# Attention in steps of two query tiles, the last output tile in two banks, and one warm-up matmul moved

## The chip, the cores and the metric

The kernel runs on one core of a Trainium2 chip. A core has a matmul engine (TensorE, PE in the profile, with its weight loads shown as PEld), a vector engine (VectorE, DVE), an activation engine (ScalarE, ACT), a general engine (GpSimd, POOL) and queues that start DMA transfers (SP's above all, shown as SPq; ACT and POOL start some too). Every engine works through its own list of instructions in order and waits at semaphores for the others. Matmul results go to PSUM, eight banks of 128 x 512 float32 here.

The metric is the device time of one execution in microseconds. The median of three runs is 651.36 (651.11 to 651.37).

## The reference

One layer of a hybrid encoder trunk in float32, one sequence of 512 rows of width 2048. One input projection gives q (8 heads of 128), k and v (2 heads each), a gate for attention, and the input and gate of a linear recurrence. Both groups are normed, gated and joined, and one output projection with a residual closes the layer.

```python
def attention_group(q, k, v, q_norm_w, k_norm_w):
    ...
    q = apply_axial_rope(rms_norm(q, q_norm_w), tables)
    k = apply_axial_rope(rms_norm(k, k_norm_w), tables)
    def block(qb):                      # 128 query rows, all heads
        s = jnp.einsum('bkgqd,bksd->bkgqs', qb, k_t) * scale
        p = jax.nn.softmax(s, axis=-1)
        return jnp.einsum('bkgqs,bksd->bkgqd', p, v_t)
...
def lru_group(xr, conv_w, conv_b, ...):  # convolution, gates, scan forward and back
    return (h_fwd + h_bwd).astype(xr.dtype)
...
# out = x + concat(norm(attn) * gate, norm(lru) * gate) @ w_out
```

## The kernel before

**Precision.** Every operand of a large product is split into a high and a low part, and each product is three matmuls (`mm3`, lines 146 to 148: high by high, high by low, low by high), so a 128 x 512 tile that sums over eight blocks takes 24 matmuls of 512 columns.

**Banks.** The eight PSUM banks are two rotating sets of four: `mm()` for scores, transposes, values and half of the outputs, `pj()` for projections and the other half of the outputs. A tile takes the bank that the tile four takes earlier in its set has used, and PE's first matmul into it waits until that older tile has been read.

**Stages.** First the input projection for the recurrence (`proj_feat`, lines from 286), then q, k and v, with the recurrence in between. Then attention, in which the projections for the gates run as filler: `weave(fill, attention(rots))` takes one step of `attention` and then as many filler pieces as it yields. One filler piece is six matmuls of 128 x 512. After attention, six more pieces and a sum of squares over heads (`group_rstd`, its matmuls at line 657). At the end the output projection, a scheme of seven products per group of columns.

**Start.** While the first chunk of x and of w_in arrives, PE is kept busy by matmuls on a tile of ones, 128 x 256 in bfloat16 (`busy`, line 942): `WARM` of them ahead of the transpose of norm_w (line 180), `WARM1` behind it, then the four transposes of x (line 233), then `WARM2`, then the first matmuls of the projection (line 294).

**Attention.** A query tile t of head h takes: `weights` (scores by `mm3`, maximum on DVE at line 576, exponential with its sum on ACT at line 579, reciprocal on DVE, scaling on POOL at line 581), `turn_weights` two steps later (four transposes at line 588, read out by ACT at line 590 and by DVE at line 591), and, one step after a head's last turn, `values` (12 matmuls, read out by DVE at line 602, squared by ACT at line 607 and summed by POOL at line 608). `turned` turns the q of the head after next (four transposes at line 536). Each step ends with `yield STEPS`, two filler pieces. Into attention also fall, among the fillers, the gates: `gate` calls four sigmoids on ACT (line 642) for each of two groups of four tiles.

PE and POOL follow the order of the code in attention; the lists of ACT, DVE and SP are set there by a scheduler. In the output stage PE, ACT, DVE and SP follow the code.

**Output.** `outputs` goes through two column groups g, each in two passes (P1, Q6, Q5, Q7, and then P2, Q3, Q4), over eight blocks i of the sum, with two tiles s of 128 rows for each product. For i from 0 to 5 the products take turns; the last two blocks are done product by product, so each product ends on its own. `take` hands banks out in turns: four from `mm`, four from `pj`. `done` reads a finished tile on DVE into the residual and stores it. The last tile of all is Q4, s = 1 of g = 1: it is read in two halves of 256 columns (line 893), both after its last matmul, and both are stored from SP's queue. Q7's tiles, in pj banks, are read at lines 877 and 879.

Of the kernel before, what the change touches and what calls it, by code (L numbers as in the profile page):

```python
# [18 lines left out]
SEQ = 512  # L19
DM = 2048  # L20
KT = DM // P
NT = SEQ // P
HD = 128
NH = 8
NKV = 2
G = NH // NKV
# [11 lines left out]
AHEAD = 600  # L38


WARM, WARM1, WARM2 = 9, 1, 4


STEPS = 2


H = 256
# [9 lines left out]
def hybrid_kernel(  # L57
# [20 lines left out]
    nc = tc.nc  # L78
# [44 lines left out]
    def b4(dt=F32, shape=(P, 2, SEQ)):  # L123
        pool, _, n = work()
        return pools[pool].tile(list(shape), dt, tag="b4", bufs=n, name=nm("b4"))
# [16 lines left out]
    def f(ap):  # L142
        return ap.bitcast(F32)
# [388 lines left out]
    def turn(rot, h):  # L532

        pt = mm()
        for t in range(NT):
            nc.tensor.transpose(pt[:, t * P : (t + 1) * P], rot[t][:, h, :], ident)  # L536
        return pt

    def split_ps(pt, hi, lo):
        nc.scalar.copy(hi, pt)  # L540
        nc.vector.tensor_sub(lo, pt, f(hi))
# [21 lines left out]
    def turned(rot, h):  # L563

        q = b4(F32R)
        split_ps(turn(rot, h), q[:, 0, :], q[:, 1, :])
        return q[:, 0, :], q[:, 1, :]

    def weights(q, g, t):

        qh, ql = q
        tt = slice(t * P, (t + 1) * P)
        sc = mm()
        mm3(sc, qh[:, tt], ql[:, tt], kth[g], ktl[g], True, True)
        mx = pools["att"].tile([P, 1], F32, tag="mx", bufs=16, name=nm("mx"))
        nc.vector.tensor_reduce(mx, sc, axis=AX.X, op=ALU.max, negate=True)  # L576
        p = k2()
        sm = pools["att"].tile([P, 1], F32, tag="sm", bufs=16, name=nm("sm"))
        nc.scalar.activation(p, sc, AF.Exp, bias=mx, accum_out=sm)
        nc.vector.reciprocal(sm, sm)  # L580
        nc.gpsimd.tensor_scalar(p, p, sm, 0.0, op0=ALU.mult, op1=ALU.add)
        return p

    def turn_weights(p, t, pth, ptl):
        tt = slice(t * P, (t + 1) * P)
        pt = mm()
        for s in range(NT):
            nc.tensor.transpose(pt[:, s * P : (s + 1) * P], p[:, s * P : (s + 1) * P], ident)  # L588
        p3 = pt.rearrange("p (s q) -> p s q", q=P)
        nc.scalar.copy(pth[:, :, tt], p3)  # L590
        nc.vector.tensor_sub(ptl[:, :, tt], p3, f(pth[:, :, tt]))

    def values(h, pth, ptl):

        gs = slice(h // G * HD, (h // G + 1) * HD)
        o = mm()
        for s in range(NT):
            mm3(o, vh[s][:, gs], vl[s][:, gs], pth[:, s, :], ptl[:, s, :], s == 0, s == NT - 1)
        if h % 2 == 0:
            ap_[h // 2] = aring.tile([P, 2, SEQ], F32, name=nm("av"))  # L600
        av, asum = ap_[h // 2][:, h % 2, :], sums["a"]
        nc.vector.tensor_copy(av, o)
        if h == 0:
            nc.scalar.activation(asum, av, AF.Square)
        else:
            sq = k2()
            nc.scalar.activation(sq, av, AF.Square)
            nc.gpsimd.tensor_add(asum, asum, sq)

    def attention(rots):  # L610

        qs, ps_, pts = {h: turned(rots[0], h) for h in range(2)}, {}, {}
        yield 13
        last = NH * NT
        for i in range(last + 3):
            h, t = divmod(i, NT)
            if i < last:
                ps_[i] = weights(qs[h], h // G, t)
                if t == 0 and h + 2 < NH:
                    qs[h + 2] = turned(rots[(h + 2) // G], (h + 2) % G)  # L620
            j = i - 3
            if j >= 0 and j % NT == NT - 1:
                values(j // NT, *pts.pop(j // NT))
            j = i - 2
            if 0 <= j < last:
                h, t = divmod(j, NT)
                if t == 0:
                    pts[h] = [
                        pools["att"].tile([P, NT, SEQ], F32R, tag="pt", bufs=ATT_PT, name=nm("pt"))
                        for _ in range(2)  # L630
                    ]
                turn_weights(ps_.pop(j), t, *pts[h])
            yield STEPS


    def gate(gs, pairs, row, sig):
# [39 lines left out]
    P1, Q6, Q5, Q7, P2, Q3, Q4 = (0, 0), (5, 5), (4, 3), (3, 4), (2, 2), (6, 1), (1, 6)  # L676
# [123 lines left out]
    PASS = (((0, "P1"), (5, "Q6"), (4, "Q5"), (3, "Q7")), ((2, "P2"), (6, "Q3"), (1, "Q4")))  # L800
    TAIL, PIECES, LAST_USE = 2, 13, 22
# [35 lines left out]
    def store(g, t, j, part=slice(0, SEQ), queue=None):  # L837

        cs = slice(j * SEQ + part.start, j * SEQ + part.stop)
        os_ = slice(2 * g * SEQ + cs.start, 2 * g * SEQ + cs.stop)  # L840
        (queue or nc.gpsimd).dma_start(of[t * P : (t + 1) * P, os_], xts[g][t][:, cs])
# [3 lines left out]
    def outputs(work):  # L845

        bank, tmp, at, held = {}, {}, [0], []

        def take(key):
            bank[key] = pj() if at[0] % 8 >= 4 else mm()  # L850
            at[0] += 1
            return bank[key]

        def tm(tag, s):
            tmp[tag, s] = fin_ev()
            return tmp[tag, s]

        def fin_ev():
            return pools["fin"].tile([P, SEQ], F32, tag="ev", bufs=4, name=nm("ev"))

        def done(g, name, s):

            xt = xts[g]
            b00, b01 = xt[s][:, :SEQ], xt[s][:, SEQ:]
            b10, b11 = xt[2 + s][:, :SEQ], xt[2 + s][:, SEQ:]
            v = nc.vector
            if name == "P1":
                nc.scalar.copy(tm("a", s), bank[name, s])
                v.tensor_add(b11, b11, tmp["a", s])
            elif name == "Q6":  # L870
                v.tensor_sub(tm("b", s), bank[name, s], tmp["a", s])
                v.tensor_sub(b01, b01, tmp["b", s])
            elif name == "Q5":
                v.tensor_add(tm("c", s), bank[name, s], tmp["b", s])
                v.tensor_add(b00, b00, tmp["c", s])
            elif name == "Q7":
                v.tensor_add(b00, bank[name, s], b00)
                store(g, s, 0)
                v.tensor_sub(b01, b01, bank[name, s])
                held.append((b10, tmp["c", s]))  # L880
            elif name == "P2":
                v.tensor_add(b11, bank[name, s], b11)
                store(g, 2 + s, 1)
            elif name == "Q3":
                v.tensor_add(b10, bank[name, s], b10)
                store(g, 2 + s, 0, queue=nc.sync if g else None)
            elif g == 0 or s == 0:
                v.tensor_add(b01, bank[name, s], b01)
                store(g, s, 1, queue=nc.sync if g else None)
            else:  # L890
                for h in range(2):
                    hs = slice(h * H, (h + 1) * H)
                    v.tensor_add(b01[:, hs], bank[name, s][:, hs], b01[:, hs])  # L893
                    store(g, s, 1, hs, nc.sync)

        def mult(use, s):

            g, second, k, i = use
            a, name = PASS[second][k]
            ah, al = mixed[i][1]  # L900
            bh, bl = ready[use]
            ts_ = slice(s * P, (s + 1) * P)
            if i == 0:
                take((name, s))
            for j, (lh, rh) in enumerate(((ah, bh), (ah, bl), (al, bh))):
                nc.tensor.matmul(  # L906
                    bank[name, s], lh[:, a, ts_], rh, start=i == 0 and j == 0,
                    stop=i == 7 and j == 2,
                )
            if i == 7:  # L910
                done(g, name, s)

        for n, use in enumerate(order_):
            g, second, k, i = use
            prepare(n + NW - 1)
            if (second, k, i) == (0, 0, 3):
                xts.setdefault(g, None)
                xts[g] = xts[g] or residual_tiles()
                residual(g)
            if second and k and held:  # L920
                b10, c = held.pop(0)
                nc.vector.tensor_add(b10, b10, c)
            if n * PIECES // LAST_USE != (n - 1) * PIECES // LAST_USE:
                next(work, None)
            if i < 8 - TAIL:
                for s in range(2):
                    mult(use, s)
            elif i == 7:
                for s in range(2):
                    for m in range(8 - TAIL, 8):  # L930
                        mult((g, second, k, m), s)

# [34 lines left out]
    for step in proj_feat(C_XR, a1, first, given):  # L969
# [8 lines left out]
        c, e = step  # L978
# [37 lines left out]
    rots = []  # L1016
# [150 lines left out]
```

## Time and profile before

| | |
|---|---|
| median of three runs | 651.36 us |
| profiled execution | 651.15 us |
| its span, first to last instruction | 649.4 us |
| PE busy | 644.0 us, 99% |
| DVE busy | 482.9 us, 74% |
| ACT busy | 345.8 us, 53% |
| POOL busy | 95.4 us, 15% |
| granted clock of PE | 1.000 |

The profile is one execution. Its span is the time from the first to the last instruction; the execution's own time is 1.8 us longer. Rows of the timeline give the start, the busy time, the engine, the line, the operation, the tiles (out<-in, without numbers) and their shape, with "x4" for four instructions in one row, and in square brackets the idle time ahead and what ended it. A matmul's busy time overlaps that of the next, so the time it costs is read from the distance of the starts, or from the chain of waits, whose rows give a start, the time it adds, and the engine and line.

### The profile page before, as it was taken

To read this page: it belongs to the slowest core of one execution; us is meant where nothing else is said; L and a number is where in the kernel's file an instruction comes from. 1 tells how busy PE (TensorE), PEld (TensorE's weight loads), DVE (VectorE), ACT (ScalarE), POOL (GpSimd) and SP (SyncE) were. 2 spreads that over 40 slices of the span, in tenths; PEclk is the share of its full clock that TensorE was granted. 3 is DMA by queue.
4 is the path that set the end of the run, shared out by engine and by line. 5 is a ranking of instruction groups with operands and counts; after the bars stand their busy time and mean duration, and the time that the engine had idled before them with its cause. 6 is when DMAs were issued, how large, how long until landed. Compare 5 with 4: busy or idle time off the path is not lost.

```text
span 649.4 us, 8581 instructions
## 1 busy us (share of the span) xinstructions
PE 644.0 (99%) x2955; PEld 532.6 (82%) x2955; DVE 482.9 (74%) x829; ACT 345.8 (53%) x639; POOL 95.4 (15%) x127
## 2 busy tenths in 40 slices
PE   9999999999999999999999999999999999999997
PEld 7888888888888888888888888888888888888885
DVE  5878679977688925855956668539967978699994
ACT  3533799489856615454744446435444754443441
POOL 0000000000012312132442435411000000010000
PEclk9999999999999999999999999999999999999999
DMA  8933243322334331446775778673354957586322
GB/s 294 323 102 111 66 138 97 98 66 66 94 101 134 97 112 33 120 139 150 173 185 142 195 145 194 152 158 92 119 174 162 333 166 247 194 280 212 119 94 97
DMA packets 53068, 96.96 MB, mean 149 GB/s; under 512 B 4317, under 2 KB 14689, under 8 KB 52897
## 3 DMA queue, kind: packets, MB, share of 16 engines
q1 hardware_dynamic: 45264, 75.17, 36.8%
q0 software_dynamic: 7056, 20.72, 13.8%
q10 hardware_dynamic: 704, 0.53, 0.3%
q8 instruction: 23, 0.38, 0.2%
q14 instruction: 21, 0.16, 0.1%
HBM read 92.21 MB, written 20.98 MB: 174 GB/s over the span
## 4 chain that ended last, share of the span: by engine, by line
PE 99%; DVE 0%; DVEq 0%; issue 0%; POOL 0%; POOLq 0%
PE pj L146 20%; PE pj L147 20%; PE pj L148 20%; PE mm L906 13%; PE pj L906 10%; PE mm L148 3%; PE mm L147 3%; PE mm L146 3%; PE mm L588 2%; PE mm L233 1%; PE pj L294 1%; PE mm L536 1%; PE mm L942 1%; PE mm L657 0%; DVE xt L893 0%; DVEq L1163 0%
## 5 line engine op out<-in xcount | busy, mean ns | idle before, releaser
L146 PE MATMUL pj<-x,wh 128*128 128x512 f32 x376 | 150.9, 401 | 0.0
L148 PE MATMUL pj<-x,wl 128*128 128x512 f32 x376 | 146.8, 390 | 0.0
L147 PE MATMUL pj<-x,wh 128*128 128x512 f32 x376 | 146.8, 390 | 0.0
L206 ACT CAST wh<-wr 128x512 fp32r<-128x512 f32 x143 | 85.5, 618 | 72.0 <-PE pj L148 25.0
L207 DVE TENSOR_TENSOR wl<-wr,wh 128x512 fp32r<-128x512 f32 x144 | 99.3, 711 | 31.0 <-ACT wh L206 31.0
L148 PEld LDWEIGHTS pj<-x,wl 128*128 128x128 f32 x376 | 70.6, 188 | 15.5
L146 PEld LDWEIGHTS pj<-x,wh 128*128 128x128 f32 x376 | 70.7, 188 | 13.8
L147 PEld LDWEIGHTS pj<-x,wh 128*128 128x128 f32 x376 | 70.8, 188 | 13.3
L720 ACT CAST oh<-rw 128x512 fp32r<-128x512 f32 x94 | 56.2, 620 | 36.7 <-PE mm L906 17.1
L146 PE MATMUL pj<-wh,x 128*128 128x512 f32 x192 | 75.0, 391 | 0.0
L147 PE MATMUL pj<-wl,x 128*128 128x512 f32 x192 | 74.8, 389 | 0.0
L148 PE MATMUL pj<-wh,x 128*128 128x512 f32 x192 | 74.8, 389 | 0.0
L721 DVE TENSOR_TENSOR ol<-rw,oh 128x512 fp32r<-128x512 f32 x94 | 61.7, 688 | 10.3 <-ACT oh L720 8.9
L906 PE MATMUL mm<-ol,mh 128*128 128x512 f32 x128 | 49.8, 389 | 0.0
L906 PE MATMUL mm<-oh,ml 128*128 128x512 f32 x128 | 49.8, 389 | 0.0
L906 PE MATMUL mm<-oh,mh 128*128 128x512 f32 x128 | 49.8, 389 | 0.0
L590 ACT CAST pt<-mm 128x512 fp32r<-128x512 f32 x32 | 18.7, 586 | 53.6 <-PE mm L588 53.6
L146 PEld LDWEIGHTS pj<-wh,x 128*128 128x128 f32 x192 | 36.0, 188 | 7.6
L148 PEld LDWEIGHTS pj<-wh,x 128*128 128x128 f32 x192 | 36.1, 188 | 7.6
L147 PEld LDWEIGHTS pj<-wl,x 128*128 128x128 f32 x192 | 36.1, 188 | 7.3
L576 DVE TENSOR_REDUCE mx<-mm 128x1 f32<-128x512 f32 x32 | 22.1, 690 | 24.3 <-PE mm L148 24.0
L906 PE MATMUL pj<-oh,ml 128*128 128x512 f32 x96 | 37.4, 389 | 0.0
(211 smaller groups left out, 1106.5 us busy)
## 6 DMA issues: line engine op xcount, KB each, us to landing
wr<-in_w_in_dram SPq DMA_DIRECT2D x71, 512.0 KB, 3.7
rw<-in_w_out_dram SPq DMA_DIRECT2D x63, 256.0 KB, 3.7
ts<-in_w_out_dram POOLq DMA_DIRECT2D x24, 512.0 KB, 6.6
rw<-ts SPq DMA_DIRECT2D x31, 256.0 KB, 4.6
ts<-ts POOLq DMA_DIRECT2D x8, 512.0 KB, 5.3
xt<-in_x_dram SPq DMA_DIRECT2D x8, 512.0 KB, 9.4
b<-in_x_dram SPq DMA_DIRECT2D x7, 512.0 KB, 8.7
out_dram<-xt POOLq DMA_DIRECT2D x12, 256.0 KB, 3.3
```

The lines of the kernel that those rows point to most:

```text
L146: nc.tensor.matmul(acc, lh, rh, start=start, stop=False)
L147: nc.tensor.matmul(acc, lh, rl, start=False, stop=False)
L148: nc.tensor.matmul(acc, ll, rh, start=False, stop=stop)
L206: rounded(hi, raw[:, k, :])
L207: nc.vector.tensor_sub(lo, raw[:, k, :], f(hi))
L233: nc.tensor.transpose(pt[:, t * P : (t + 1) * P], xc[:, t, ks], ident)
L576: nc.vector.tensor_reduce(mx, sc, axis=AX.X, op=ALU.max, negate=True)
L588: nc.tensor.transpose(pt[:, s * P : (s + 1) * P], p[:, s * P : (s + 1) * P], ident)
L590: nc.scalar.copy(pth[:, :, tt], p3)
L720: nc.scalar.copy(hi, src)
L721: nc.vector.tensor_sub(lo, src, f(hi))
L906: nc.tensor.matmul(bank[name, s], lh[:, a, ts_], rh, start=i == 0 and j == 0, stop=i == 7 and j == 2,)
```

## The change

Three parts.

1. `WARM, WARM1` go from 9, 1 to 10, 0: the warm-up matmul that stood between the transpose of norm_w and the transposes of x stands ahead of both.
2. Attention goes in steps d of two query tiles. A step does the values of a head whose turns are complete (even d from 4 on), then the turns of two tiles of weights from the step before last, then in odd d up to 11 the turn of q, then a score tile, one filler piece, a score tile, three filler pieces. The last values yield no filler; 85 pieces lie within attention instead of 83, and six instead of eight after the last values.
3. The last output tile is summed in two banks of 256 columns each: half 0 in the mm bank of the tile before, half 1 in the next bank in turn, a pj bank. Each matmul of 512 columns becomes two of 256 with the same weights. Within the last two blocks half 0 comes first, so it is complete six matmuls ahead of half 1. Half 0 is stored from SP's queue, half 1 from ACT's.

```diff
-WARM, WARM1, WARM2 = 9, 1, 4
-STEPS = 2
+WARM, WARM1, WARM2 = 10, 0, 4
+STEPS = 1, 3
...
-        last = NH * NT
-        for i in range(last + 3):
-            h, t = divmod(i, NT)
-            if i < last:
-                ps_[i] = weights(qs[h], h // G, t)
-                if t == 0 and h + 2 < NH:
-                    qs[h + 2] = turned(rots[(h + 2) // G], (h + 2) % G)
-            j = i - 3
-            if j >= 0 and j % NT == NT - 1:
-                values(j // NT, *pts.pop(j // NT))
-            j = i - 2
...
-                turn_weights(ps_.pop(j), t, *pts[h])
-            yield STEPS
+        for d in range(2 * NH + 3):
+            h, half = divmod(d - 4, 2)
+            if h >= 0 and half == 0:
+                values(h, *pts.pop(h))
+            h, half = divmod(d - 2, 2)
+            if 0 <= h < NH:
...
+                for t in (2 * half, 2 * half + 1):
+                    turn_weights(ps_.pop((h, t)), t, *pts[h])
+            h, half = divmod(d, 2)
+            if h < NH:
+                if half == 1 and h + 2 < NH:
+                    qs[h + 2] = turned(rots[(h + 2) // G], (h + 2) % G)
+                for e, t in enumerate((2 * half, 2 * half + 1)):
+                    ps_[h, t] = weights(qs[h], h // G, t)
+                    yield STEPS[e]
+            elif d < 2 * NH + 2:
+                yield sum(STEPS)
+            else:
+                yield 0
...
-            else:
-                for h in range(2):
-                    hs = slice(h * H, (h + 1) * H)
-                    v.tensor_add(b01[:, hs], bank[name, s][:, hs], b01[:, hs])
-                    store(g, s, 1, hs, nc.sync)
+                hs = slice(half * H, (half + 1) * H)
+                v.tensor_add(b01[:, hs], bank[name, s, half][:, :H], b01[:, hs])
+                store(g, s, 1, hs, (nc.sync, nc.scalar)[half])
...
+            if half is None:
+                key, to, cols = (name, s), slice(0, SEQ), slice(0, SEQ)
+            else:
+                key, to, cols = (name, s, half), slice(0, H), slice(half * H, (half + 1) * H)
             if i == 0:
-                take((name, s))
+                take(key)
             for j, (lh, rh) in enumerate(((ah, bh), (ah, bl), (al, bh))):
                 nc.tensor.matmul(
-                    bank[name, s], lh[:, a, ts_], rh, start=i == 0 and j == 0,
+                    bank[key][:, to], lh[:, a, ts_], rh[:, cols], start=i == 0 and j == 0,
...
+            for s in range(2):
+                last = g == 1 and PASS[second][k][1] == "Q4" and s == 1
+                for half in (0, 1) if last else (None,):
+                    for m in range(8 - TAIL, 8) if i == 7 else (i,) if i < 8 - TAIL else ():
+                        mult((g, second, k, m), s, half)
```

The code that follows the first changed lines stands four or more lines further down, so that line 906 before is line 913 after, and lines 877 and 879 are 881 and 883.

On PE in attention, before, ahead of the fifth score tile's fillers: a score tile (`mm_568`), the turn of q into `mm_573`, one turn of weights into `mm_574`, and then the fillers' projection tile. The names in brackets are the semaphores that an instruction waits for; "x3" is three equal instructions.

```order
L146 MATMUL mm_568_2779<-kt_447_2202,b4_510_2508 128x512 [waits Activation_49]
L147 MATMUL mm_568_2779<-kt_447_2202,b4_510_2508 128x512
L148 MATMUL mm_568_2779<-kt_447_2202,b4_510_2508 128x512
L536 MATMUL mm_573_2791<-ident_81,ev_400_2032 128x128 [waits DVE_49]
L536 MATMUL mm_573_2791<-ident_81,ev_401_2034 128x128
L536 MATMUL mm_573_2791<-ident_81,ev_402_2036 128x128
L536 MATMUL mm_573_2791<-ident_81,ev_403_2038 128x128
L588 MATMUL mm_574_2798<-ident_81,k2_553_2710 128x128 [waits DVE_49,Pool_49]
L588 MATMUL mm_574_2798<-ident_81,k2_553_2710 128x128 x3
```

The same engine after, in the step d = 3: two turns of weights (`mm_581`, `mm_582`), the turn of q (`mm_584`), and a first score tile (`mm_585`). The step's second score tile, `mm_589`, stands six matmuls further down with a wait for DVE.

```order
L588 MATMUL mm_581_2838<-ident_81,k2_553_2710 128x128 [waits DVE_49,Pool_49]
L588 MATMUL mm_581_2838<-ident_81,k2_553_2710 128x128 x3
L588 MATMUL mm_582_2845<-ident_81,k2_557_2727 128x128 [waits DVE_49,Pool_49]
L588 MATMUL mm_582_2845<-ident_81,k2_557_2727 128x128 x3
L536 MATMUL mm_584_2853<-ident_81,ev_400_2032 128x128 [waits Activation_49]
L536 MATMUL mm_584_2853<-ident_81,ev_401_2034 128x128
L536 MATMUL mm_584_2853<-ident_81,ev_402_2036 128x128
L536 MATMUL mm_584_2853<-ident_81,ev_403_2038 128x128
L146 MATMUL mm_585_2860<-kt_447_2202,b4_510_2508 128x512 [waits Activation_49]
```

Twelve transposes stand in one group there, eight in most other steps.

On PE in the first round (i = 0) of the last pass, before: Q4's two tiles, `mm_1287` and `mm_1288`, and then the next block's P2.

```order
L906 MATMUL mm_1287_5875<-oh_1265_5787,mh_871_4215 128x512 [waits DVE_49,Activation_49]
L906 MATMUL mm_1287_5875<-ol_1266_5788,mh_871_4215 128x512
L906 MATMUL mm_1287_5875<-oh_1265_5787,ml_872_4216 128x512
L906 MATMUL mm_1288_5879<-oh_1265_5787,mh_871_4215 128x512 [waits DVE_49]
L906 MATMUL mm_1288_5879<-ol_1266_5788,mh_871_4215 128x512
L906 MATMUL mm_1288_5879<-oh_1265_5787,ml_872_4216 128x512
L906 MATMUL pj_1277_5844<-oh_1271_5813,mh_874_4237 128x512 [waits Activation_49]
```

And after: `mm_1288` has 256 columns, and `pj_1289`, the second half, follows it.

```order
L913 MATMUL mm_1288_5879<-oh_1265_5787,mh_871_4227 128x256 [waits DVE_49]
L913 MATMUL mm_1288_5879<-ol_1266_5788,mh_871_4227 128x256
L913 MATMUL mm_1288_5879<-oh_1265_5787,ml_872_4228 128x256
L913 MATMUL pj_1289_5883<-oh_1265_5787,mh_871_4227 128x256 [waits DVE_49]
L913 MATMUL pj_1289_5883<-ol_1266_5788,mh_871_4227 128x256
L913 MATMUL pj_1289_5883<-oh_1265_5787,ml_872_4228 128x256
L913 MATMUL pj_1277_5844<-oh_1271_5813,mh_878_4245 128x512 [waits Activation_49]
```

The first matmul of `pj_1289` has a wait for DVE that no instruction had there before. It is for DVE's reads of Q7's first tile, `pj_1182`, whose bank it takes; after the change DVE's list at that place is, as it was before but for line numbers:

```order
L725 TENSOR_TENSOR ol_1272_5814<-rw_1269_5809,oh_1271_5813 128x512 [waits DMAHW0_49,Activation_49]
L799 TENSOR_TENSOR tc_1164_5407<-tc_1164_5407,rw_1269_5809 128x512
L725 TENSOR_TENSOR ol_1274_5819<-rw_1270_5811,oh_1273_5818 128x512 [waits DMAHW1_49,Activation_49]
L881 TENSOR_TENSOR xt_1211_5572<-pj_1182_5456,xt_1211_5572 128x512 [waits PE_49]
L883 TENSOR_TENSOR xt_1211_5572<-xt_1211_5572,pj_1182_5456 128x512
```

So the second half of the last tile starts behind the second read of `pj_1182`; nothing else moved there.

More of the change, by code (lines that the diff above doesn't have):

```diff
@@ L613, in attention @@
         yield 13
-        last = NH * NT
-        for i in range(last + 3):
-            h, t = divmod(i, NT)
-            if i < last:
-                ps_[i] = weights(qs[h], h // G, t)
-                if t == 0 and h + 2 < NH:
-                    qs[h + 2] = turned(rots[(h + 2) // G], (h + 2) % G)
-            j = i - 3
-            if j >= 0 and j % NT == NT - 1:
-                values(j // NT, *pts.pop(j // NT))
-            j = i - 2
-            if 0 <= j < last:
-                h, t = divmod(j, NT)
-                if t == 0:
+        for d in range(2 * NH + 3):
[4 more added lines that the diff above has]
+            if 0 <= h < NH:
+                if half == 0:
                     pts[h] = [
@@ L859, in fin_ev, with done @@
             return pools["fin"].tile([P, SEQ], F32, tag="ev", bufs=4, name=nm("ev"))
-        def done(g, name, s):
+        def done(g, name, s, half=None):
             xt = xts[g]
@@ L886, in done @@
                 store(g, 2 + s, 0, queue=nc.sync if g else None)
-            elif g == 0 or s == 0:
+            elif half is None:
                 v.tensor_add(b01, bank[name, s], b01)
@@ L890, in done, with mult @@
             else:
-                for h in range(2):
-                    hs = slice(h * H, (h + 1) * H)
-                    v.tensor_add(b01[:, hs], bank[name, s][:, hs], b01[:, hs])
-                    store(g, s, 1, hs, nc.sync)
-        def mult(use, s):
+                hs = slice(half * H, (half + 1) * H)
+                v.tensor_add(b01[:, hs], bank[name, s, half][:, :H], b01[:, hs])
+                store(g, s, 1, hs, (nc.sync, nc.scalar)[half])
+        def mult(use, s, half=None):
             g, second, k, i = use
@@ L910, in mult @@
             if i == 7:
-                done(g, name, s)
+                done(g, name, s, half)
         for n, use in enumerate(order_):
@@ L924, in outputs @@
                 next(work, None)
[L925 to L931, printed above, removed]
+            for s in range(2):
[3 more added lines that the diff above has]
+                        mult((g, second, k, m), s, half)
     ctx.enter_context(tc.manual_schedule(engines={mybir.EngineType.PE}))
```

## The prediction

> **What bounds the kernel now.** I read the page's shares first, then the chain of waits.
>
> ```profile
> span 649.4 us, 8581 instructions
> PE 644.0 (99%) x2955; PEld 532.6 (82%) x2955; DVE 482.9 (74%) x829; ACT 345.8 (53%) x639; POOL 95.4 (15%) x127
> PE 99%; DVE 0%; DVEq 0%; issue 0%; POOL 0%; POOLq 0%
> ...
> 525.50 5.44 PE mm L906 x24
> ```
>
> TensorE (PE) is busy 99% of the span and 99% of the chain. So only three things count: the time of PE's own instructions, any new wait of PE, and the few tenths behind its last matmul. The chain's row of 24 gives the unit: 5.44/24 = 0.2267 us for a 128x512 matmul. The sum below is made against the profiled execution, 651.15 us; the median of the three runs, 651.36, is 0.21 above it. A difference under 0.2% (1.3 us) counts here as no change, about what a measurement of this kernel can tell.
>
> **Transposes in attention.** Next I read PE's timeline in the attention. No idle time stands at any row there.
>
> ```profile
> 300.03 0.60 PE L588 MATMUL mm<-ident,k 128*128 128x128 f32 x4
> ...
> 307.83 0.60 PE L536 MATMUL mm<-ident,ev 128*128 128x128 f32 x4
> 308.26 0.60 PE L588 MATMUL mm<-ident,k 128*128 128x128 f32 x4
> ...
> 312.12 0.60 PE L588 MATMUL mm<-ident,k 128*128 128x128 f32 x4
> ...
> 374.83 0.60 PE L588 MATMUL mm<-ident,k 128*128 128x128 f32 x4
> ...
> 378.73 0.60 PE L588 MATMUL mm<-ident,k 128*128 128x128 f32 x4
> ...
> 382.63 0.60 PE L588 MATMUL mm<-ident,k 128*128 128x128 f32 x4
> ...
> 307.99 0.44 PE mm L536 x4
> ```
>
> The step from 378.73 to 382.63 is 3.90 us and holds, beside its four transposes, 15 matmuls (12 of the filler, 3 of the scores): 15 × 0.2267 = 3.40, so four transposes cost 0.50. The step from 307.83 to 312.12 holds the same 15 and eight transposes back to back: 4.29 − 3.40 = 0.89. Four more cost 0.39 to 0.44 (the chain's row), so a group has a price of its own, some 0.1. Twelve in one group should cost 0.89 + 0.44 = 1.33.
>
> Before, the 32 turns of weights and the 6 turns of q stand as 28 groups of four and 5 of eight: 28 × 0.50 + 5 × 0.89 = 18.45. After, the order gives one group of four, 11 of eight and 5 of twelve: 0.50 + 9.79 + 6.65 = 16.94. That is **−1.5 us**; I take **−1.4**, since a step without rounding comes to 0.497. Ends: −1.75 if further transposes cost 0.39, −0.95 if part of a group's price grows with its length. Score, value and filler matmuls stay as many as before.
>
> **What waits in attention.** Four mm banks rotate. In a step with 12 transposes the second score tile takes the bank of the first turn, which ACT and DVE must have read out.
>
> ```profile
> 418.55 0.60 PE L588 MATMUL mm<-ident,k 128*128 128x128 f32 x4
> 419.19 0.59 ACT L590 CAST pt<-mm 128x512 fp32r<-128x512 f32 x1 [0.90 <-PE mm L588]
> 419.81 0.69 DVE L591 TENSOR_TENSOR pt<-mm,pt 128x512 fp32r<-128x512 f32 x1 [0.27 <-ACT pt L590]
> ...
> 317.44 1.14 ACT L642 ACTIVATE k<-ev 128x512 f32<-128x512 f32 x2
> 318.60 1.28 ACT L579 ACT_TABLE_LOAD   x1
> ...
> 355.49 1.08 POOL L754 DMA_DIRECT2D ts<-in_w_out_dram  x1 [7.37 <-DVE sm L580]
> 356.10 1.21 POOL L581 TENSOR_SCALAR k<-k,sm 128x512 f32<-128x512 f32 x1
> ```
>
> The bank is free 419.81 + 0.69 − 418.55 = 1.95 us after the first transpose. After the change 12 transposes (1.33), a score tile (0.68) and one filler (1.36) stand between: 3.37, so 1.4 us are left. Only the step in which the first gate's four sigmoids and their table load stand ahead of that read-out on ACT eats this: two sigmoids take 1.14 and a load 1.28, so four and a load 3.6 us. The gate's tiles are ready some two microseconds ahead of that turn, so part of the 3.6 lies before it and about 1.5 behind it, as much as is left. I take **+0.15** (0 to +0.6). In the step of the second gate there is no turn of q, so no such wait. POOL's scaling of p (356.10) already sits behind DMA starts that wait for earlier landings; before, p is turned two steps, some 7.8 us, after its score, afterwards two double steps, some 15 us: 0. The step with the sums is hidden behind the two scores' fillers.
>
> **The end of attention** loses two of eight fillers between the last values and the sum of squares.
>
> ```profile
> 427.90 0.69 DVE L602 COPY av<-mm 128x512 f32<-128x512 f32 x1 [2.93 <-PE mm L148]
> 428.68 0.63 ACT L607 ACTIVATE k<-av 128x512 f32<-128x512 f32 x1 [4.44 <-DVE av L602]
> 429.46 1.53 POOL L608 TENSOR_TENSOR asum<-asum,k 128x512 f32<-128x512 f32 x1
> 438.58 0.94 PE L657 MATMUL mm<-ones,asum 128*128 128x1 f32 x8
> ```
>
> The sum is there at 430.99, 3.1 us after the values; six fillers are 36 × 0.2267 = 8.2 us. 5 us are left: 0. The two fillers run earlier, they are not dropped.
>
> **The warm-up matmul moved ahead.**
>
> ```profile
> 1.13 2.10 PE mm L942 x9
> ...
> 3.16 0.28 PE L180 MATMUL mm<-ident,nw_st 16*128 16x16 f32 x1
> 3.37 0.39 PE L942 MATMUL mm<-ones 128*128 128x256 bf16 x1
> 3.56 1.09 PE L233 MATMUL mm<-ident,b 128*128 128x128 f32 x4
> ...
> 5.50 1.99 PE pj L294 x4
> ...
> 7.92 3.19 PE pj L294 x14
> ```
>
> Ten in a row end at 1.13 + 10 × 2.10/9 = 3.46, the turn of norm_w follows (0.21 in the chain), and the x transposes start at 3.67 against a start of 3.56: between them nothing is added or removed. I take 0 (−0.1 to +0.1). The clock is still low for the first real matmuls (1.99/4 = 0.50 each) and full from 7.92 (3.19/14 = 0.23). The Trainium skill ("TensorE: Matmul & The Clock Gate", section "What's actually happening") says that the clock is released after a busy window of some 3.4 us that runs free of the program; no run here shows that, and by it a moved matmul could shift the release by chance. That is a rival below.
>
> **The last tile in halves.** 24 matmuls of 512 columns become 48 of 256, each with its own load of weights. Their columns alone cost the same, 48 × 0.1133 = 5.44. A load takes up to 0.44/4 = 0.11 (the transposes, which stand back to back at that rate), so it hides by a hair. I take +0.2 (a fixed part of 4 ns each); ends 0 and +0.56 (0.125 each). The Trainium skill's page just named, section "LDWEIGHTS (loading the stationary operand)", gives 107 ns for 128 columns, and "Back-to-back issue gap" 109 ns for a matmul of 256; its sustained 81 ns for pairs of 128 the trace contradicts with 0.11. By these figures the estimate would be −0.2 instead of +0.2.
>
> Now the wait. The second half takes a pj bank, the one that held Q7's first tile. PE reaches its first matmul in the first round of the second pass, right behind P2, Q3 and Q4's first three. It must wait until DVE has read Q7's tile, in `v.tensor_sub(b01, b01, bank[name, s])` at line 879.
>
> ```profile
> 605.03 0.69 DVE L869 TENSOR_TENSOR xt<-xt,ev 128x512 f32<-128x512 f32 x1 [0.66 <-ACT ev L868]
> ...
> 616.03 0.69 DVE L877 TENSOR_TENSOR xt<-pj,xt 128x512 f32<-128x512 f32 x1
> 616.63 0.68 DVE L879 TENSOR_TENSOR xt<-xt,pj 128x512 f32<-128x512 f32 x1
> ...
> 612.38 0.39 PE L906 MATMUL pj<-oh,mh 128*128 128x512 f32 x1
> ...
> 615.78 0.39 PE L906 MATMUL mm<-oh,mh 128*128 128x512 f32 x1
> ...
> 616.23 0.39 PE L906 MATMUL mm<-oh,ml 128*128 128x512 f32 x1
> 616.46 0.39 PE L906 MATMUL pj<-oh,mh 128*128 128x512 f32 x1
> ```
>
> DVE works without a gap worth naming from 605.03 on, and in the order its instructions there are the same as before, so it ends line 879 at 616.63 + 0.68 = 617.31 in this clock. PE is due at 615.78 + 3 × 0.1133 = 616.12. The wait is 1.19 and a handover of about 0.1: **+1.3 us** (1.15 to 1.5; nothing if DVE should be ahead). Behind the waiting matmul stands all of PE's remaining work, so it counts in full. It comes once. The first half's bank is that of the old tile and brings no new wait.
>
> **The end.**
>
> ```profile
> 644.79 0.39 PE L906 MATMUL mm<-oh,ml 128*128 128x512 f32 x1
> 645.22 0.76 DVE L893 TENSOR_TENSOR xt<-mm,xt 128x256 f32<-128x256 f32 x2 [0.67 <-PE mm L906]
> 645.67 0.81 SPq L841 DMA_DIRECT2D out_dram<-xt  x2
> ...
> 645.22 0.42 DVE xt L893
> ```
>
> Before, both half-additions (0.76) and two stores one behind the other on SP's queue (0.81) follow the last matmul. After, the first half is complete six matmuls earlier and is added and stored under the second; one addition (0.42) and one store on ACT's idle queue are left: 0.76 − 0.42 = 0.34, or 0.41 by the second issue. I take **−0.33** (−0.15 to −0.40).
>
> **Sum:** −1.4 + 0.15 + 0 + 0.2 + 1.3 − 0.33 = −0.1: 651.05 for the profiled execution, 651.25 against the median. I forecast 651.2, no change.
>
> **Rivals.** *No bank wait* (faster): DVE reads Q7's tile before 616.1. For it speaks that DVE's start of this stretch depends on ACT (0.66 idle at 605.03) and a small shift there would move it; against it, that PE and DVE's distance has 1.2 us to close. Time: 651.25 − 1.3 = 649.95. *The group's price is per transpose* (0.50 per four however grouped): no gain in attention, 651.25 + 1.4 = 652.65; the rows 307.83 to 312.12 speak against it. *Loads not hidden* (slower): if a load of weights waits for the matmul ahead where that has only 256 columns, each costs 0.11 + 0.113, and 48 cost 10.7 instead of 5.6: 651.25 + 5.1 = 656.3. It decides as soon as a load takes longer than 0.113; the transposes' 0.11 leave 3%. *Read-outs late in most double steps* (slower): if ACT or DVE is over 1.4 us late in five of them, at 0.4 us each, +2.0: 653.2; their gaps of 0.27 to 4.4 us in the rows above speak against it. *The clock released later or earlier*: four matmuls at 0.50 instead of 0.23 are 1.1 us, 650.1 or 652.3.
>
> **How the numbers follow.** The forecast 0.61; no bank wait 0.17; price per transpose 0.06; loads 0.06; late read-outs 0.07; the clock 0.03. From 649.9 to 652.8 leaves out the loads, the late read-outs and a few tenths of the forecast's far ends; the likeliest case alone spans 650.4 to 652.2. Faster takes no bank wait and the low end of the forecast, 0.19; slower takes loads, late read-outs and half of the price per transpose, 0.19; no change 0.62.
>
> **What would show it.** A step of two query tiles (30 matmuls) should be 7.69 us without a turn of q and 8.13 with one, and idle on PE in attention should stand at one score tile at most. An idle of about 1.2 us should stand ahead of one 128x256 matmul in a pj bank, released by DVE's subtraction in Q7. The 128x256 matmuls should start 0.113 to 0.12 apart, and one DVE addition should follow the last. The prediction is wrong if that idle is missing or repeated, or if the halves start 0.2 apart.

## The result, and the profile after

The changed kernel is slower: 653.14 us median of 13 runs (652.13 to 654.11) against 651.31 (651.11 to 652.45), a ratio of 1.0026 with a 95% interval of 1.0017 to 1.0034. The forecast was 651.2, no change. A second set of ten runs (experiment e10) gave 652.53 and 1.0016 (1.0007 to 1.0026). The profiled execution took 652.40, its span is 650.6; of the first set only two runs were faster.

The page of the changed kernel, and its list of PE's waits (who waits for whom, us in total, times, the longest):

```profile
span 650.6 us, 8628 instructions
PE 644.1 (99%) x2979; PEld 534.7 (82%) x2979; DVE 481.1 (74%) x829; ACT 349.1 (54%) x639; POOL 98.5 (15%) x127
PE 96%; DVE 2%; issue 1%; DMA 0%; ACT 0%; POOL 0%; DVEq 0%; POOLq 0%
```

```profile
PE mm L947 <- POOL ones L154: 1.1, 1, 1.1
PE pj L913 <- DVE xt L883: 1.1, 1, 1.1
PE mm L146 <- DVE pt L591: 0.3, 1, 0.3
```

PE's share of the chain fell from 99% to 96%. The first wait stood before too; the other two are new: the forecast wait for Q7's bank, and the wait of a second score tile for DVE's read-out. The places, in PE's and DVE's timelines:

```profile
317.00 0.40 PE L148 MATMUL pj<-x,wl 128*128 128x512 f32 x1
317.72 0.50 PE L146 MATMUL mm<-kt,b 128*128 128x512 f32 x1 [0.33 <-DVE pt L591]
...
402.17 0.49 PE L146 MATMUL mm<-kt,b 128*128 128x512 f32 x1
402.50 0.40 PE L147 MATMUL mm<-kt,b 128*128 128x512 f32 x1
...
615.72 0.28 PE L913 MATMUL mm<-oh,ml 128*128 128x256 f32 x1
617.07 0.39 PE L913 MATMUL pj<-oh,mh 128*128 128x256 f32 x1 [1.07 <-DVE xt L883]
617.29 0.28 PE L913 MATMUL pj<-ol,mh 128*128 128x256 f32 x1
...
616.33 0.68 DVE L883 TENSOR_TENSOR xt<-xt,pj 128x512 f32<-128x512 f32 x1
```

A bracket counts from the modelled end of the matmul ahead, so what a wait costs is read from the starts. From 615.72 to 617.07 are 1.35 instead of 0.12: 1.23. The next is 0.22 behind instead of 0.12. At the first gate the starts are 0.72 apart instead of 0.23, 0.5 lost, and at the second gate (402.17) 0.33, 0.1 lost.

The chain of waits gives the stages:

```profile
8.02 3.21 PE pj L294 x14
...
344.10 0.87 PE mm L588 x8
...
351.80 0.87 PE mm L588 x8
...
362.69 0.87 PE mm L588 x8
...
525.21 5.44 PE mm L913 x24
...
645.93 0.73 PE pj L913 x6
646.66 0.02 issue
646.68 0.42 DVE xt L896
```

The row of 14 starts 0.10 later than before, and the row of 24 in the output stage 0.29 earlier (525.50 before). So attention gained 0.39 in this execution. PE's last matmul ends at 646.66 against 645.19, 1.47 later: the output stage lost 1.76. Behind it remain 650.6 − 646.66 = 3.94 against 649.4 − 645.19 = 4.21: 0.27 gained. The sum is 0.10 − 0.39 + 1.76 − 0.27 = +1.2, as the two executions' own times are apart (652.40 − 651.15 = 1.25). The median is 0.7 higher than this execution; the experiments look for that too.

### The profile page after: what moved, and what is told of

It reads as the page before. It is cut to its first block, busy times and chain, and to the rows that moved or that the text cites. A ratio compares the mean times of both kernels' runs of the same rounds, so it can differ in the third digit from the quotient of the medians.

```text
span 650.6 us, 8628 instructions
## 1 busy us (share of the span) xinstructions
PE 644.1 (99%) x2979; PEld 534.7 (82%) x2979; DVE 481.1 (74%) x829; ACT 349.1 (54%) x639; POOL 98.5 (15%) x127
## 4 chain that ended last, share of the span: by engine, by line
PE 96%; DVE 2%; issue 1%; DMA 0%; ACT 0%; POOL 0%; DVEq 0%; POOLq 0%
PE pj L148 20%; PE pj L146 20%; PE pj L147 20%; PE mm L913 12%; PE pj L913 10%; PE mm L146 3%; PE mm L148 3%; PE mm L147 3%; PE mm L588 2%; PE mm L233 1%; PE pj L294 1%; PE mm L536 1%; PE mm L947 0%; DMA rw<-in_w_out_dram 0%; DVE ol L725 0%
## 5 line engine op out<-in xcount | busy, mean ns | idle before, releaser
L146 PE MATMUL pj<-x,wh 128*128 128x512 f32 x376 | 147.6, 392 | 0.0
L147 PE MATMUL pj<-x,wh 128*128 128x512 f32 x376 | 146.4, 389 | 0.0
L207 DVE TENSOR_TENSOR wl<-wr,wh 128x512 fp32r<-128x512 f32 x144 | 96.3, 695 | 36.0 <-ACT wh L206 35.1
L913 PE MATMUL mm<-oh,ml 128*128 128x512 f32 (+1 forms) x128 | 48.9, 382 | 0.0
L913 PE MATMUL mm<-ol,mh 128*128 128x512 f32 (+1 forms) x128 | 48.9, 382 | 0.0
L913 PE MATMUL mm<-oh,mh 128*128 128x512 f32 (+1 forms) x128 | 48.9, 382 | 0.0
L913 PE MATMUL pj<-oh,mh 128*128 128x512 f32 (+1 forms) x104 | 39.8, 383 | 1.1 <-DVE xt L883 1.1
L913 PE MATMUL pj<-ol,mh 128*128 128x512 f32 (+1 forms) x104 | 39.7, 382 | 0.0
L913 PE MATMUL pj<-oh,ml 128*128 128x512 f32 (+1 forms) x104 | 39.6, 381 | 0.0
```

Source lines behind the costliest of these rows:

```text
L146: nc.tensor.matmul(acc, lh, rh, start=start, stop=False)
L147: nc.tensor.matmul(acc, lh, rl, start=False, stop=False)
L207: nc.vector.tensor_sub(lo, raw[:, k, :], f(hi))
L913: nc.tensor.matmul(bank[key][:, to], lh[:, a, ts_], rh[:, cols], start=i == 0 and j == 0, stop=i == 7 and j == 2,)
```

## The experiments

The first four ask which part costs what, and where the runs' spread (2 us, against 0.5 for all but one run of the kernel before in the same set) comes from.

**e1, attention alone.**

```diff
-WARM, WARM1, WARM2 = 10, 0, 4
+WARM, WARM1, WARM2 = 9, 1, 4
...
-        def done(g, name, s, half=None):
+        def done(g, name, s):
```

(and the rest of the output stage as before)

> Attention in double steps alone, warm-up and last tile as before. By the trace of the changed kernel the stretch of attention became 0.40 us shorter, with waits of 0.6 us at the first gate and 0.1 us at the second. Theory A (the spread of the changed kernel's runs, 652.1 to 654.1, comes from these waits in attention): median 651.3 to 652.2, runs spread over more than 1 us. Theory B (the spread comes from the output stage, where PE now waits for a saturated DVE): median 650.9, runs within 0.5 us of each other, like those of the kernel before.

Measured: 651.08 (650.11 to 652.47) against 651.27, ratio 0.9997 (0.9988 to 1.0006). The median lies just under A's range and the spread is A's. Its profiled execution was one of its longest, 652.22, and shows why:

```profile
317.07 0.40 PE L148 MATMUL pj<-x,wl 128*128 128x512 f32 x1
318.25 0.50 PE L146 MATMUL mm<-kt,b 128*128 128x512 f32 x1 [0.78 <-DVE pt L591]
...
402.49 0.39 PE L148 MATMUL pj<-x,wl 128*128 128x512 f32 x1
403.53 0.50 PE L146 MATMUL mm<-kt,b 128*128 128x512 f32 x1 [0.66 <-DVE av L602]
```

Here the same two waits cost 0.95 and 0.81 us, against 0.5 and 0.1 in the profile above, from the same instructions in the same order. The second one is released by DVE's copy of the values: in a step with values, the second score tile takes their bank.

**e2, the last tile alone.**

```diff
-WARM, WARM1, WARM2 = 10, 0, 4
-STEPS = 1, 3
+WARM, WARM1, WARM2 = 9, 1, 4
+STEPS = 2
...
-        for d in range(2 * NH + 3):
+        for i in range(last + 3):
```

(and the rest of attention as before)

> The last tile in two banks alone, attention and warm-up as before. By the trace the output stage became 1.77 us longer (bank wait 1.24, a load of weights behind it 0.11, slower matmuls 0.41) and the end 0.24 us shorter: +1.5. Theory A: median 652.8, runs within 0.5 us of each other. Theory B: median 652.8 to 653.5, runs spread over more than 1 us.

Measured: 652.95 (652.40 to 654.15), 1.0027 (1.0017 to 1.0036). The price of +1.68 holds, a little over the 1.5 of the trace. The spread is B's, not A's.

**e3, the whole change with fillers 2 and 2.**

```diff
-STEPS = 1, 3
+STEPS = 2, 2
```

> The whole change, but with fillers split 2 and 2 between and behind the two score tiles, so that the second score tile comes 1.36 us later behind the first turn. Theory A: the waits for DVE in attention (0.6 and 0.1 us) go, median 652.2 to 652.5, spread down to 0.5 us. Theory B: median lower by 0.7 at most and the spread stays over 1 us.

Measured: 652.24 (651.87 to 652.89), 1.0013 (1.0004 to 1.0022). That is 0.9 under the changed kernel's first set and 0.3 under its second. The median is where A has it; the spread of 1.0 is narrower, but twice what A expected, and the waits did not all go: the profile keeps one at the first gate, 0.2 in the list of waits and 0.36 by the starts.

**e4, the second half of the last tile one round later.**

```diff
-                    for m in range(8 - TAIL, 8) if i == 7 else (i,) if i < 8 - TAIL else ():
+                    first = () if half == 1 and i == 0 else (0, 1) if half == 1 and i == 1 else (i,)
+                    for m in range(8 - TAIL, 8) if i == 7 else first if i < 8 - TAIL else ():
```

> The whole change, but the second half of the last tile skips the first round and does the blocks 0 and 1 in the second round, four microseconds later: same matmuls, and Q7's bank has long been read. Both theories: no wait of PE for DVE's Q7 subtraction, 1.35 us less at the median, 651.8. Theory A: spread stays over 1 us. Theory B: spread falls to 0.5 us and the median falls by up to 2 us, to 651.1.

Measured: 651.44 (650.49 to 652.72), 1.0001 (0.9992 to 1.0010), 1.7 under the changed kernel's first set and 1.1 under its second, where 1.35 was expected. PE's list of waits has no wait in the output stage, and the half follows without a pause:

```profile
619.86 0.28 PE L913 MATMUL mm<-oh,ml 128*128 128x256 f32 x1
619.98 0.29 PE L913 MATMUL pj<-oh,mh 128*128 128x256 f32 x1
```

From the row of 24 (525.41) to the end of PE's last matmul (645.69) the output stage is 0.59 longer than before, instead of 1.76. So the bank wait is shown, and it was about two thirds of what the last tile cost PE. Summing both halves in one bank, which would need no further bank, was not tried. The spread stayed over 1 us, which A expected and B did not.

Taken together the spreads don't decide between A and B. e2 and later e9, whose attention is that of the kernel before, spread over more than 1.7 us as well, and so does the kernel before itself in some sets (650.68 to 652.91 beside e5). Part of the spread arises ahead of everything that differs in attention and output: in the fourteen profiles on record the first four matmuls at line 294 take 1.16 to 2.08 us in all, and the group of eight transposes of x behind the first projection matmuls starts anywhere from 10.43 to 11.15, with the warm-up matmul moved (10.68 to 11.08) or not (10.43 to 11.15). So what the waits cost is read from the profiles, and those of the second score tile are of other length in each.

**e5, POOL scales one column.** The next question is why DVE reads out so late at the gates. The timelines of DVE and POOL there, first for the changed kernel at both gates, then for e1 at the second:

```profile
313.49 1.11 DVE L650 SCALAR_TENSOR_TENSOR ev<-ev,vec,k 128x512 f32<-128x512 f32 x1
314.52 1.28 DVE L207 TENSOR_TENSOR wl<-wr,wh 128x512 fp32r<-128x512 f32 x2
...
312.22 1.83 POOL L581 TENSOR_SCALAR k<-k,sm 128x512 f32<-128x512 f32 x2
...
388.49 2.44 DVE L650 SCALAR_TENSOR_TENSOR ev<-ev,vec,k 128x512 f32<-128x512 f32 x1
390.85 1.69 DVE L207 TENSOR_TENSOR wl<-wr,wh 128x512 fp32r<-128x512 f32 x2
...
387.75 1.78 POOL L608 TENSOR_TENSOR asum<-asum,k 128x512 f32<-128x512 f32 x1
389.03 2.36 POOL L581 TENSOR_SCALAR k<-k,sm 128x512 f32<-128x512 f32 x2
```

```profile
389.03 3.28 DVE L650 SCALAR_TENSOR_TENSOR ev<-ev,vec,k 128x512 f32<-128x512 f32 x1
...
389.14 1.78 POOL L608 TENSOR_TENSOR asum<-asum,k 128x512 f32<-128x512 f32 x1
390.40 2.36 POOL L581 TENSOR_SCALAR k<-k,sm 128x512 f32<-128x512 f32 x2
```

The same gate product takes 1.11, 2.44 and 3.28 us, the long ones while POOL sums and scales beside it. Those POOL instructions stand behind DMA starts (lines 755 and 758), some of which wait for an earlier landing by the profile (7.5 us in two of them, 2.8 in three), and they fall at another place beside DVE's list in each execution. The edit leaves out the scaling of 511 of 512 columns; the lists of PE, ACT and DVE stay word for word.

```diff
-        nc.gpsimd.tensor_scalar(p, p, sm, 0.0, op0=ALU.mult, op1=ALU.add)
+        nc.gpsimd.tensor_scalar(p[:, :1], p[:, :1], sm, 0.0, op0=ALU.mult, op1=ALU.add)
```

> The whole change, but POOL scales one column of each tile of weights instead of 512 (the scaling of the others is left out, so the attention is not normalised); the lists of PE, ACT and DVE are the same. Theory P: the waits of PE at the two gates are long and uneven because POOL's scalings, let go by DMA landings, run beside DVE's gate products and splits and stretch them (a product 2.4 and 3.3 us instead of 0.75, a pair of splits 1.69 instead of 1.28). Then without them the waits at both gates together are 0.1 to 0.3 us, the median falls by 0.7 to 1.0, to 652.1 to 652.4, and the runs lie within about 0.8 of each other. Theory Q: the order of ACT's and DVE's lists at the gates makes the waits, whatever POOL does: waits of 0.6 us or more and a median of 653.1 stay.

Measured: 652.03 (651.45 to 653.30), 1.0013 (1.0004 to 1.0022), 1.1 under the changed kernel's first set and 0.5 under its second. Theory P holds for the waits. For the spread it does not: the runs lie within 1.85 us, not 0.8, so the scalings are not the whole of it. The rows:

```profile
313.71 0.75 DVE L650 SCALAR_TENSOR_TENSOR ev<-ev,vec,k 128x512 f32<-128x512 f32 x1
314.38 1.29 DVE L207 TENSOR_TENSOR wl<-wr,wh 128x512 fp32r<-128x512 f32 x2
...
317.22 0.40 PE L148 MATMUL pj<-x,wl 128*128 128x512 f32 x1
317.59 0.50 PE L146 MATMUL mm<-kt,b 128*128 128x512 f32 x1
...
388.38 1.25 DVE L650 SCALAR_TENSOR_TENSOR ev<-ev,vec,k 128x512 f32<-128x512 f32 x1
```

The gate product takes 0.75, the pair of splits 1.29, and the second score tile starts 0.37 instead of 0.23 behind the filler: a wait of 0.14. At the second gate POOL's sum of squares is still there and the product takes 1.25 (0.75 at the first); no wait of PE is left there. So POOL's scaling makes the waits long and uneven; the order of ACT's and DVE's lists alone makes 0.14.

**e10, the changed kernel once more.** There is no edit.

> The changed kernel itself once more, for a second profiled execution. If POOL's scalings make the waits at the gates, the bank wait in the last pass is again 1.24 and the waits of the second score tile at the gates have other lengths than 0.6 and 0.1, between 0.1 and 1.0 each, going with the durations of DVE's gate products. If the waits are the same to 0.05, the spread has another source.

Measured: 652.53 (651.48 to 653.56), 1.0016 (1.0007 to 1.0026); the profiled execution took 653.00.

```profile
312.88 2.37 POOL L581 TENSOR_SCALAR k<-k,sm 128x512 f32<-128x512 f32 x2
...
313.64 1.15 DVE L650 SCALAR_TENSOR_TENSOR ev<-ev,vec,k 128x512 f32<-128x512 f32 x1
314.71 1.69 DVE L207 TENSOR_TENSOR wl<-wr,wh 128x512 fp32r<-128x512 f32 x2
...
317.14 0.40 PE L148 MATMUL pj<-x,wl 128*128 128x512 f32 x1
318.32 0.50 PE L146 MATMUL mm<-kt,b 128*128 128x512 f32 x1 [0.78 <-DVE pt L591]
```

POOL's pair starts 0.66 later than in the first profile (312.22), DVE's product only 0.15 later, so the pair now runs beside the splits too, which take 1.69 instead of 1.28. The wait costs 0.95 instead of 0.5. At the second gate the starts are 0.30 apart, 0.07 lost, a little less than the 0.1 expected. The bank wait is again 1.1 in the list.

**e7, the warm-up matmul alone.**

```diff
-WARM, WARM1, WARM2 = 9, 1, 4
+WARM, WARM1, WARM2 = 10, 0, 4
```

> The warm-up matmul moved alone. By the trace the x transposes started 0.02 to 0.1 later: 651.3, no difference that can be told, by both theories. If it were worth 0.5 either way, the sum of the other parts would have to be read anew.

Measured: 651.13 (650.88 to 651.46), 0.9998 (0.9989 to 1.0007). It is worth nothing that can be told.

**e9, the kernel before with the last store on ACT's queue.**

```diff
-                    store(g, s, 1, hs, nc.sync)
+                    store(g, s, 1, hs, (nc.sync, nc.scalar)[h])
```

> The kernel before with one edit: the second half of the last tile is stored from ACT's queue instead of SP's; the matmuls and additions are as before. If the gain of 0.24 at the end of the changed kernel came from the queue, the span behind the last matmul falls by up to 0.2 and the median to about 651.1; if it came from the first half's earlier addition, nothing changes: 651.25.

Measured: 651.25 (650.81 to 652.64), 1.0002 (0.9993 to 1.0010). The queue is worth nothing that can be told. That leaves the first half's earlier addition for what the end gained; no run has it alone.

**e6 and e11, attention alone with fillers 2 and 2; e12, with 1 and 3 again.** e6 and e11 are e1 with one more edit, e12 is e1:

```diff
-STEPS = 1, 3
+STEPS = 2, 2
```

> Attention in double steps with fillers 2 and 2, warm-up and last tile as before. From the whole change with 2 and 2 (652.24) less the price of the last tile (652.95 - 651.27 = 1.68): 650.55, faster than the kernel before by 0.7; runs within 1 us of each other.

> Attention in double steps with fillers 2 and 2 once more, to see whether it beats the kernel before on another set of runs: 650.3 to 650.6 against 651.2, with one wait of 0.1 to 0.6 at the first gate in the profile. If the first result was a chance of the chip, the median lies within 0.2 of the kernel before.

> Attention in double steps with fillers 1 and 3 once more, beside 2 and 2 on the same chip: by the waits at the gates 0.5 to 0.9 slower than with 2 and 2, so 650.9 to 651.4, and wider spread; if the two splits differ by less than 0.2 at the median, the wait of the second score tile is not what 2 and 2 saves.

Measured: e6 650.40 (650.12 to 652.84), 0.9990 (0.9981 to 0.9999); e11 650.78 (650.21 to 651.85), 0.9992 (0.9982 to 1.0001); e12 651.30 (650.25 to 652.87), 1.0000 (0.9990 to 1.0010). On one chip 2 and 2 is 0.5 under 1 and 3. It is also 0.4 to 0.8 under the kernel before, the one version that seems to beat it, though one of its two intervals just holds 1. Two expectations failed: e6's runs spread over 2.7 us instead of 1, and e11's median lies between its two cases. The split doesn't remove the wait at the first gate: by the starts it costs 0.37 in e6, and 1.00 in e11, where a sum and a gate product ahead of the read-outs take 0.90 and 1.16 us instead of 0.68 and 0.75, beside POOL's scaling. At the second gate e3, e6 and e11 lose nothing; with 1 and 3 five profiles lose 0 to 0.81 there.

**e8, fillers 3 and 1.** This is e1 too, with one edit:

```diff
-STEPS = 1, 3
+STEPS = 3, 1
```

> Attention in double steps with fillers 3 and 1, warm-up and last tile as before: the second score tile comes 1.36 later still than with 2 and 2, which has one wait of 0.37 left at the first gate. If the distance of the second score tile from the first turn is what makes the waits, none is left and the median is 650.0 to 650.4. If the next first turn now comes too early behind the second score tile (one filler between), other waits appear at the turns and the median is 650.6 or more.

Measured: 655.72 (653.87 to 656.64, five runs), 1.0065 (1.0052 to 1.0078). The second expectation holds, at a size it did not foresee. The profiled execution was the shortest of the five, 653.87; what the others lose beyond it no trace shows.

```profile
394.15 1.94 DVE L650 SCALAR_TENSOR_TENSOR ev<-ev,vec,k 128x512 f32<-128x512 f32 x2 [1.19 <-ACT k L646]
...
397.22 0.68 DVE L591 TENSOR_TENSOR pt<-mm,pt 128x512 fp32r<-128x512 f32 x1
397.82 1.28 DVE L207 TENSOR_TENSOR wl<-wr,wh 128x512 fp32r<-128x512 f32 x2
399.02 0.68 DVE L591 TENSOR_TENSOR pt<-mm,pt 128x512 fp32r<-128x512 f32 x1
...
396.58 0.39 PE L148 MATMUL pj<-x,wl 128*128 128x512 f32 x1
398.04 0.47 PE L146 MATMUL mm<-pt,v 128*128 128x512 f32 x1 [1.08 <-DVE pt L591]
399.75 0.50 PE L147 MATMUL mm<-pt,v 128*128 128x512 f32 x1 [1.24 <-DVE pt L591]
```

At the second gate the values wait for the last two read-outs of the turns, 1.2 and 1.5 us. In the list that the scheduler made of this split, those read-outs stand on DVE behind two gate products, which wait for ACT's sigmoids, and the second one behind a pair of splits too. So the split of the fillers moves more than the second score tile: it gives ACT and DVE other lists. That holds for 2 and 2 as well, so its gain is not shown to be the distance alone.

## Why the prediction was wrong

By its own steps:

- **The warm-up, 0.** Right as far as can be told (e7). The start does vary by 0.7 us from profile to profile, but with the matmul moved or not, so this belongs to the spread and not to the change.
- **The transposes, −1.4.** The mechanism was right, the term too large. The chain's rows give 351.80 − 344.10 = 7.70 for a double step without a turn of q, and with 30 matmuls (6.80) a group of eight costs 0.90. From 351.80 to 362.69 stand 42 matmuls (9.52): 1.37 for twelve. The sum is 0.50 + 11 × 0.90 + 5 × 1.37 = 17.25, a saving of 1.2 against 18.45. Whole profiles show 1.0: attention gained 0.39 in the changed kernel's with 0.6 of waits in it, and 0.83 in e5's with 0.14 (from the first turns of q, at 254.79 before and 255.10 in e5, to the row of 24, at 525.50 and 524.98).
- **The wait in attention, +0.15 (0 to +0.6).** This is the step that failed. Without POOL's scaling it is 0.14 (e5). With it, in five profiles with fillers 1 and 3, the first gate costs 0.37 (e12), 0.50 (the changed kernel), 0.90 (e4) and 0.95 (e1 and e10). To 0.02 this is each time 0.14 and what the gate product and the pair of splits ahead take beyond e5's: 0.21, 0.35, 0.75, 0.80 and 0.80. At the second gate the prediction had "no turn of q, so no such wait". It overlooked that with values in the step the second score tile stands four mm tiles behind them, and e1 lost 0.81 there, e12 0.74, the other three 0 to 0.1. Both gates together cost 1.1 on average of the five profiles. For POOL it asked only whether its scalings come in time for the turns, which they did, and not what they do to DVE meanwhile. The nearest rival, late read-outs in most double steps, was right in kind: one or two steps were late, by up to 1 us each. That its time, 653.2, is nearly the measured one is chance, since it counted five late steps at 0.4. So attention makes about −1.0 + 1.1 = +0.1 instead of −1.25, and its two sets alone lie at −0.19 (e1, 651.08) and +0.09 (e12, 651.30).
- **The bank wait, +1.3.** Right, in its place, releaser and size: 1.23 and 0.1 on the matmul behind it. The rival without it fell.
- **The halves' matmuls, +0.2.** Too small. The chain's row of six takes 0.73, 0.12 each instead of 0.1133: 48 × 0.0067 = 0.3, and the 512-column matmuls behind them add some 0.1. That is 1.76 − 1.33 = 0.4 in all; in e4, without the bank wait, the stage is 0.59 longer. Whether the load of weights or a fixed part makes it, no run tells apart; the 0.4 lies within the bounds given, e4's 0.59 just above them.
- **The end, −0.33.** −0.27, and none that can be told from the queue (e9).

The two parts of the last tile that were off make +0.3, attention some 1.3: 0.9 by the waits and 0.4 by the transposes. Measured part by part the change is +1.4 (e2 +1.68, e1 −0.19, e7 −0.08), between the two sets of the whole change (+1.83 and +1.24).

## What to carry to other kernels

When PE has no slack, each bank handed out once more takes the place of a tile that someone must have read: find its reader in the order, its end in the trace, and the price is there before anything is built. A margin of 1.4 us in front of a wait must hold for the longest form of the instructions ahead, and here those were longest beside POOL's sums and scalings (a product of 0.75 us took up to 3.28): look for POOL's rows beside DVE's before counting with a DVE duration from elsewhere. Where a scheduler sets some of the lists, a shift of filler work changes them too, and has to be measured as a change of its own.

## What the runs showed of the hardware

A DVE product of two tiles, 128 x 512, took 0.75 us without POOL's full scalings and sum (e5) and 0.97 (e12) to 3.28 (e1) with them beside it; the splits beside them took 1.69 a pair instead of 1.28. The Trainium skill ("SBUF — State Buffer", section "SBUF: two separate sides") has DVE and POOL share a port pair that one of them holds for a whole instruction, also for a DVE instruction with two SBUF inputs against a POOL one that reads SBUF. The sizes agree: 3.28 is 0.75 and some 2.5 us, and from the start of POOL's sum (389.14) to about the end of its first scaling (390.40 + 2.36/2) are 2.4. The order does not quite: in the profile the product starts 0.1 ahead of the sum and is stretched all the same; POOL's rows are rough, so which of them held the port first is not shown.
